# Encoder trunk on one core: next head's queries and the first attention projection moved ahead of the recurrences

## The chip, the cores and the metric

One core of one Trainium2 chip runs the whole kernel. The metric is the device time in microseconds (us) of one execution; three timed runs stand for the kernel before, and one further execution was profiled. TensorE is PE, its weight load PEld, VectorE DVE, ScalarE ACT, GpSimd POOL, SyncE SP.

## What is computed

Two layers, 1024 positions of width 1024, fp32. The reference, cut:

```python
def hybrid_layer(x, ...):
    proj = rms_norm(x, norm1_g) @ w_in
    mq, mk, mv, mo, mi, mf, aq, ak, av = split(proj)
    mq, mk = silu(centred_depthwise_conv([mq, mk], conv_w))       # width 5
    # mLSTM, 4 heads x 128: one chunkwise scan forward, one backward, summed
    hm = mlstm_chunkwise(q, k, v, gi[0], log_sigmoid(gf[0])) + flip(mlstm_chunkwise(flip(...)))
    y_m = head_rms_norm(hm) * head_norm_g * sigmoid(mo)
    # attention, 8 heads x 64: rotary q and k, windows (128,1) (512,4) (2048,16), merged
    y_a = dilated_attention(rope(aq), rope(ak), av)
    x = x + [y_m, y_a] @ w_out
    u = relu(rms_norm(x, norm2_g) @ w_up)
    return x + (u * u) @ w_down
```

## The kernel before, in words

**Matmuls.** Everything is kept transposed: 128 features on the partitions, 1024 positions along the free dimension, in two halves of 512. Each fp32 product is three matmuls of split operands, a high part and a residue (`mm3`, L85 to L92): `wh` with `hh`, `wh` with `hl`, `wl` with `hh`. Weights come by DMA in tiles `wr` of four 128x128 blocks; `wsplit` (L76) has ScalarE cast the high part `wh` (L80) and GpSimd subtract it, which leaves the residue `wl` (L82). There are three buffers each of `wr`, `wh` and `wl`. One projection to 128 features (`proj`, L184) needs two such tiles and is 48 matmuls of 128x512, in two PSUM banks (`pj`, at times `pm`).

**mLSTM** (L291 to L442, called from `layer`, L692). For each of the four heads: `m_proj` projects q and k and lets each go through a width-5 convolution (ScalarE's first product, L317; four VectorE passes over 128x1024, L319) and SiLU (L335, L337), transposes v, and projects the output gate `so` (L339 its sigmoid). `m_values` projects the v of the next head; head 0's was made with the gates. `m_head` fetches two broadcasts per direction by DMA (L351 to L358), makes the decay matrix E from them (L353, L355), transposes k (L369, copied to `kn`, L371), makes the scores (L376) and multiplies them into E (L378, VectorE); then it runs the recurrence over 8 chunks in both directions (L392, L394, L403; VectorE updates the state C, L406 and L408). `m_tail` normalises the head before, transposes it (L438) and multiplies it into `y`. The transposes, the scores and the recurrence's updates share two PSUM banks, tag `s`.

**Attention** (from L452). After the four heads `a_kq` projects k and then q of the first pair of heads, with the rotation on VectorE and GpSimd (`rope`, L462 to L469); it is a generator, and each step is three matmuls. v follows. Then there is `a_pair` for each of four pairs: 8 turns T of scores, softmax, transposes (L639) and products; between them `fill(n)` draws n steps of the next pair's projections, so that TensorE has work while VectorE and ScalarE make the softmax.

**Output projection and feed-forward** use seven products of block sums (Strassen's scheme), with `products` (L831): four weight tiles `w`, each 12 matmuls over four k-tiles whose operands are in `parts`: `parts[0]` holds k-tiles 0 and 1, `parts[1]` 2 and 3. The operands of the output projection's first product are casts `b<-y` (L792) of the results `y`.

**Order of the work.** A scheduler places the instructions on each engine's queue; its priority is the program's order, raised by 400 for weight splits and PSUM evacuations, and `issue_after` ties an instruction behind another one. In `a_pair` PE keeps the written order (`in_order`). Each engine then runs its queue in order, and waits for the others by semaphores.

Of the kernel before, what the change touches and what calls it, by code (L numbers as in the profile page):

```python
# [19 lines left out]
P = 128  # L20
# [23 lines left out]
class Trunk:  # L44
# [152 lines left out]
    def gates(self, L, hs, acc, pl, order):  # L197
# [3 lines left out]
        ws = self.ws0 or [self.wload(self.a["w_in"][L, 0, :, 4 * i:4 * i + 4]) for i in range(2)]  # L201
        yield
# [3 lines left out]
        self.ws0 = None  # L206
# [84 lines left out]
    def m_values(self, L, h, hs, r, mp):  # L291
# [8 lines left out]
        return zv, v1  # L300

    def m_proj(self, L, h, hs, r, mp, gates, values):

        nc = self.nc
        base = 1 + 4 * h
        zv, v1 = values
        qk = []
        for i in range(2):
            ps = self.proj(L, base + 1 + i, hs)
            z = mp.tile([P, S + 4], F32, name="z", tag="z", bufs=3)  # L310
            nc.gpsimd.memset(z[:, 0:2], 0.0)
            nc.gpsimd.memset(z[:, S + 2:S + 4], 0.0)
            for t in range(2):
                self.evac_r(z[:, 2 + t * HALF:2 + (t + 1) * HALF], ps[t], r, t)
            c = mp.tile([P, S], F32, name="c", tag="qk", bufs=4)
            cw = self.cw[:, L, i * MH + h]
            nc.scalar.activation(c, z[:, 0:S], AF.Copy, scale=cw[:, 0:1])  # L317
            for j in range(1, 5):
                nc.vector.scalar_tensor_tensor(out=c, in0=z[:, j:j + S], scalar=cw[:, j:j + 1], in1=c,  # L319
                                               op0=ALU.mult, op1=ALU.add)  # L320
            qk.append(c)
            if i == 1:
                next(gates, None)
            else:
                for g in range(2):
                    pt = self.mx.tile([P, 4, P], F32, name="pt", tag="s", bufs=2)
                    for c in range(4):
                        nc.tensor.transpose(pt[:, c], zv[:, (4 * g + c) * P:(4 * g + c + 1) * P], self.ident)
                    nc.scalar.copy(v1[:, 4 * g:4 * g + 4, 0:P], pt)
        so = mp.tile([P, S], F32, name="so", tag=f"so{h % 2}", bufs=1)  # L330
        ps = self.proj(L, base, hs)
# [3 lines left out]
        last = nc.scalar.activation(qk[1], qk[1], AF.Silu)  # L335
        with self.tc.issue_after(last.ins):
            last = nc.scalar.activation(qk[0], qk[0], AF.Silu)  # L337
# [253 lines left out]
    def a_pair(self, p, qkv, ops, ap, more, nxt=None):  # L591
# [58 lines left out]
        if p == 0:  # L650
            fill(8)
            v1, v23 = self.a_vt(qkv[2], ap, fill)
# [560 lines left out]
```

## Time and profile before

| | us |
|---|---|
| three runs, median (lowest to highest) | 2574.28 (2572.6 to 2579.54) |
| profiled execution, whole time | 2581.37 |
| its span in the trace | 2579.6 |
| busy in it: PE, PEld | 2451.5, 1954.0 |
| busy in it: DVE, ACT, POOL | 1897.8, 1241.0, 1342.9 |

The span holds what the trace shows of the execution; the rest of the whole time lies around it. Layer 0's mLSTM is at about 25 to 282 us, its attention to 582, the output projection from there; in layer 1 the mLSTM lies at 1275 to 1553, the attention from 1594, the output projection from 1858. A row of the timeline gives the start, the duration, and in brackets the time for which the engine was idle before it, with what ended that wait. The granted clock is a share of full speed, 2.4 GHz.

### The profile page before, as it was taken

To read this page: it belongs to the slowest core of one execution; us is meant where nothing else is said; L and a number is where in the kernel's file an instruction comes from. 1 tells how busy PE (TensorE), PEld (TensorE's weight loads), DVE (VectorE), ACT (ScalarE), POOL (GpSimd) and SP (SyncE) were. 2 spreads that over 40 slices of the span, in tenths; PEclk is the share of its full clock that TensorE was granted. 3 is DMA by queue.
4 is the path that set the end of the run, shared out by engine and by line. 5 is a ranking of instruction groups with operands and counts; after the bars stand their busy time and mean duration, and the time that the engine had idled before them with its cause. 6 is when DMAs were issued, how large, how long until landed. Compare 5 with 4: busy or idle time off the path is not lost. (4 is left out here: it accounts for less than half of the span.)

```text
span 2579.6 us, 35988 instructions
## 1 busy us (share of the span) xinstructions
PE 2451.5 (95%) x13470; PEld 1954.0 (76%) x13470; DVE 1897.8 (74%) x2388; ACT 1241.0 (48%) x2068; POOL 1342.9 (52%) x1111
## 2 busy tenths in 40 slices
PE   8999989998999999999998999999999999999997
PEld 6788766666788788787787887666677787887876
DVE  6576766778886766968766666667787968778687
ACT  5444444455544545454543443445466455454554
POOL 4232323336676667767642324223366767667765
PEclk9999999999999999999999999999999999999998
DMA  4432100154565555655333221003454555545553
GB/s 146 120 88 85 39 22 26 46 144 109 104 108 113 107 106 103 111 107 122 90 107 102 86 82 36 21 25 95 107 119 95 110 107 112 115 101 106 111 102 82
DMA packets 136288, 239.65 MB, mean 93 GB/s; under 512 B 15009, under 2 KB 34481, under 8 KB 136113
## 3 DMA queue, kind: packets, MB, share of 16 engines
q0 software_dynamic: 49216, 101.45, 23.5%
q1 hardware_dynamic: 86896, 135.89, 17.1%
q8 instruction: 107, 1.75, 0.3%
q14 instruction: 69, 0.56, 0.1%
HBM read 228.50 MB, written 8.65 MB: 92 GB/s over the span
## 5 line engine op out<-in xcount | busy, mean ns | idle before, releaser
L82 POOL TENSOR_TENSOR wl<-w,wh 128x512 fp32r<-128x512 f32 x484 | 774.0, 1619 | 287.7 <-ACT wh L80 286.7
L846 PE MATMUL ph<-b,wh 128*128 128x512 f32 x2240 | 692.8, 391 | 2.0 <-ACT wh L80 2.0
L80 ACT CAST wh<-w 128x512 fp32r<-128x512 f32 x484 | 297.9, 618 | 401.7 <-POOL wl L82 121.7
L846 PEld LDWEIGHTS ph<-b,wh 128*128 128x128 f32 x2240 | 421.6, 188 | 90.9 <-ACT wh L80 3.9
L846 PE MATMUL ph<-b,wl 128*128 128x512 f32 x1120 | 440.9, 394 | 14.9 <-POOL wl L82 14.5
L82 POOL TENSOR_TENSOR wl<-wr,wh 128x512 fp32r<-128x512 f32 x132 | 197.3, 1496 | 395.0 <-ACT wh L80 365.4
L846 PE MATMUL pj<-b,wh 128*128 128x512 f32 x1224 | 381.2, 393 | 9.3 <-ACT wh L80 4.7
L793 DVE TENSOR_TENSOR b<-T,b 128x1024 fp32r<-128x1024 f32 x144 | 248.4, 1729 | 122.6 <-ACT b L792 119.0
L90 PE MATMUL pj<-hh,wh 128*128 128x512 f32 x768 | 312.9, 407 | 0.6 <-ACT wh L80 0.6
L92 PE MATMUL pj<-hh,wl 128*128 128x512 f32 x768 | 301.7, 393 | 0.2 <-POOL wl L82 0.2
L91 PE MATMUL pj<-hl,wh 128*128 128x512 f32 x768 | 301.5, 393 | 0.0
L846 PEld LDWEIGHTS pj<-b,wh 128*128 128x128 f32 x1224 | 231.6, 190 | 60.5 <-ACT wh L80 5.6
L846 PEld LDWEIGHTS ph<-b,wl 128*128 128x128 f32 x1120 | 210.9, 188 | 71.1 <-POOL wl L82 28.2
L846 PE MATMUL pj<-b,wl 128*128 128x512 f32 x612 | 241.1, 394 | 11.1 <-POOL wl L82 11.1
L90 PEld LDWEIGHTS pj<-hh,wh 128*128 128x128 f32 x768 | 145.2, 189 | 44.3 <-issue 16.8
L792 ACT CAST b<-T 128x1024 fp32r<-128x1024 f32 x144 | 151.4, 1051 | 50.5 <-DVE T L808 17.1
L92 PEld LDWEIGHTS pj<-hh,wl 128*128 128x128 f32 x768 | 145.0, 189 | 32.2 <-POOL wl L82 1.3
L91 PEld LDWEIGHTS pj<-hl,wh 128*128 128x128 f32 x768 | 145.1, 189 | 27.1 <-issue 0.5
L820 POOL DMA_DIRECT2D w<-w_down x128 | 117.0, 946 | 73.4 <-DMA w<-w_down 27.2
L626 ACT ACTIVATE sm<-sm,nm 128x512 f32<-128x512 f32 x128 | 91.6, 717 | 127.9 <-DVE nm L624 127.9
L846 PEld LDWEIGHTS pj<-b,wl 128*128 128x128 f32 x612 | 116.0, 190 | 39.1 <-POOL wl L82 15.1
L820 POOL DMA_DIRECT2D w<-w_up x128 | 113.5, 908 | 61.6 <-POOL wl L82 22.9
(264 smaller groups left out, 4383.1 us busy)
## 6 DMA issues: line engine op xcount, KB each, us to landing
w<-w_up SPq DMA_DIRECT2D x128, 256.0 KB, 2.7
w<-w_up POOLq DMA_DIRECT2D x128, 256.0 KB, 4.1
w<-w_down SPq DMA_DIRECT2D x128, 256.0 KB, 2.7
w<-w_down POOLq DMA_DIRECT2D x128, 256.0 KB, 4.2
wr<-w_in SPq DMA_DIRECT2D x116, 256.0 KB, 2.7
E<-cm SPq DMA_DIRECT2D x16, 512.0 KB, 6.1
qi<-gd SPq DMA_DIRECT2D x16, 512.0 KB, 7.4
E<-gd POOLq DMA_DIRECT2D x16, 512.0 KB, 7.5
```

Of the source, the lines that this page charges most:

```text
L80: self.split = nc.scalar.copy(wh, raw).ins
L82: nc.gpsimd.tensor_tensor(out=wl, in0=raw, in1=wh.bitcast(F32), op=ALU.subtract)
L90: nc.tensor.matmul(ps, wh[:, j, :], xh[:, sl], start=start, stop=False)
L91: nc.tensor.matmul(ps, wh[:, j, :], xl[:, sl], start=False, stop=False)
L92: nc.tensor.matmul(ps, wl[:, j, :], xh[:, sl], start=False, stop=stop)
L626: nc.scalar.activation(sm, sm, AF.Exp, scale=-1.0, bias=nm, accum_out=l)
L792: nc.scalar.copy(hi, src)
L793: nc.vector.tensor_tensor(out=lo, in0=src, in1=hi.bitcast(F32), op=ALU.subtract)
L820: self.nc.gpsimd.dma_start(w, src, accum_op=ALU.add)
L846: nc.tensor.matmul(out, a[:, k, :], b, start=new and k + i == 0, stop=k + i == 5, skip_group_check=not new)
```

## The change

It has five parts. (1) `m_first` takes the place of `m_values`: beside the next head's v it projects the next head's q, with q's convolution and the transposes of v, and it is called before `m_head`; `m_proj` keeps k and the gate. (2) For the last head the first 16 steps of `a_kq`, the k projection of the first pair, are drawn before `m_head`. (3) In the first pair, `fill(8)` ahead of the transposes of v becomes `fill(6)`, and turns 0 to 2 draw 5 steps where they drew 4. (4) The output projection's first products run over `parts[0]` for three weight tiles and then over `parts[1]` (`late`). (5) Layer 1's gate weights are loaded and split ahead of the norm in the program's order.

```diff
@@ -198,12 +198,10 @@
 
         nc = self.nc
         ps = [self.mx.tile([P, HALF], F32, name="ps", tag="s", bufs=2) for _ in range(2)]
-        ws = self.ws0 or [self.wload(self.a["w_in"][L, 0, :, 4 * i:4 * i + 4]) for i in range(2)]
-        yield
+        ws = self.ws0
         for k in order:
             for t in range(2):
                 self.mm3(ps[t], ws[k // 4], k % 4, hs[k], t, k == order[0], k == order[-1])
-        self.ws0 = None
         ws = [self.wload(self.a["w_in"][L, 4, :, 4 * i:4 * i + 4]) for i in range(2)]
         self.ahead = self.pj2(True)
         for t in range(2):
@@ -288,7 +286,24 @@
         yield
 
 
-    def m_values(self, L, h, hs, r, mp):
+    def m_conv(self, L, h, i, hs, r, mp):
+
+        nc = self.nc
+        ps = self.proj(L, 2 + 4 * h + i, hs)
+        z = mp.tile([P, S + 4], F32, name="z", tag="z", bufs=3)
+        nc.gpsimd.memset(z[:, 0:2], 0.0)
+        nc.gpsimd.memset(z[:, S + 2:S + 4], 0.0)
+        for t in range(2):
+            self.evac_r(z[:, 2 + t * HALF:2 + (t + 1) * HALF], ps[t], r, t)
+        c = mp.tile([P, S], F32, name="c", tag="qk", bufs=4)
+        cw = self.cw[:, L, i * MH + h]
+        nc.scalar.activation(c, z[:, 0:S], AF.Copy, scale=cw[:, 0:1])
+        for j in range(1, 5):
+            nc.vector.scalar_tensor_tensor(out=c, in0=z[:, j:j + S], scalar=cw[:, j:j + 1], in1=c, op0=ALU.mult,
+                                           op1=ALU.add)
+        return c
+
+    def m_first(self, L, h, hs, r, mp):
 
         nc = self.nc
         ps, self.ahead = self.ahead or self.proj(L, 4 + 4 * h, hs), None
@@ -297,48 +312,32 @@
             self.evac_r(zv[:, t * HALF:(t + 1) * HALF], ps[t], r, t)
         v1 = mp.tile([P, NC, P + 1], F32, name="v1", tag=f"v1{h % 2}", bufs=1)
         nc.gpsimd.memset(v1[:, :, P:P + 1], 1.0)
-        return zv, v1
-
-    def m_proj(self, L, h, hs, r, mp, gates, values):
-
-        nc = self.nc
-        base = 1 + 4 * h
-        zv, v1 = values
-        qk = []
-        for i in range(2):
-            ps = self.proj(L, base + 1 + i, hs)
-            z = mp.tile([P, S + 4], F32, name="z", tag="z", bufs=3)
-            nc.gpsimd.memset(z[:, 0:2], 0.0)
-            nc.gpsimd.memset(z[:, S + 2:S + 4], 0.0)
-            for t in range(2):
-                self.evac_r(z[:, 2 + t * HALF:2 + (t + 1) * HALF], ps[t], r, t)
-            c = mp.tile([P, S], F32, name="c", tag="qk", bufs=4)
-            cw = self.cw[:, L, i * MH + h]
-            nc.scalar.activation(c, z[:, 0:S], AF.Copy, scale=cw[:, 0:1])
-            for j in range(1, 5):
-                nc.vector.scalar_tensor_tensor(out=c, in0=z[:, j:j + S], scalar=cw[:, j:j + 1], in1=c,
-                                               op0=ALU.mult, op1=ALU.add)
-            qk.append(c)
-            if i == 1:
-                next(gates, None)
-            else:
-                for g in range(2):
-                    pt = self.mx.tile([P, 4, P], F32, name="pt", tag="s", bufs=2)
-                    for c in range(4):
-                        nc.tensor.transpose(pt[:, c], zv[:, (4 * g + c) * P:(4 * g + c + 1) * P], self.ident)
-                    nc.scalar.copy(v1[:, 4 * g:4 * g + 4, 0:P], pt)
+        q = self.m_conv(L, h, 0, hs, r, mp)
+        for g in range(2):
+            pt = self.mx.tile([P, 4, P], F32, name="pt", tag="s", bufs=2)
+            for c in range(4):
+                nc.tensor.transpose(pt[:, c], zv[:, (4 * g + c) * P:(4 * g + c + 1) * P], self.ident)
+            nc.scalar.copy(v1[:, 4 * g:4 * g + 4, 0:P], pt)
+        return q, v1
+
+    def m_proj(self, L, h, hs, r, mp, gates, first):
+
+        nc = self.nc
+        q, v1 = first
+        k = self.m_conv(L, h, 1, hs, r, mp)
+        next(gates, None)
         so = mp.tile([P, S], F32, name="so", tag=f"so{h % 2}", bufs=1)
-        ps = self.proj(L, base, hs)
+        ps = self.proj(L, 1 + 4 * h, hs)
         for t in range(2):
             self.evac_r(so[:, t * HALF:(t + 1) * HALF], ps[t], r, t)
         next(gates, None)
-        last = nc.scalar.activation(qk[1], qk[1], AF.Silu)
+        last = nc.scalar.activation(k, k, AF.Silu)
         with self.tc.issue_after(last.ins):
-            last = nc.scalar.activation(qk[0], qk[0], AF.Silu)
+            last = nc.scalar.activation(q, q, AF.Silu)
         with self.tc.issue_after(last.ins):
             last = nc.scalar.activation(so, so, AF.Sigmoid)
         self.tables(last)
-        return qk[0], qk[1], so, v1
+        return q, k, so, v1
 
     def m_head(self, L, h, prj, nat, mp, pend):
         nc = self.nc
@@ -648,7 +647,7 @@
             return p1s
 
         if p == 0:
-            fill(8)
+            fill(6)
             v1, v23 = self.a_vt(qkv[2], ap, fill)
         sms = weights(0)
         if p > 0:
@@ -662,7 +661,7 @@
                 ahead = weights(T + 1)
             if late:
                 take1(*late)
-            fill((5 if p > 0 else 4) if not last else 3)
+            fill((5 if p > 0 or T < 3 else 4) if not last else 3)
             if T % 4 == 0:
                 o1 = self.mx.tile([P, 4, P], F32, name="o1", tag="o", bufs=1)
             late = T, o1, turn(T, sms)
@@ -693,6 +692,9 @@
         tc, nc, a = self.tc, self.nc, self.a
         self.L = L
         order = (0, 1, 2, 3, 4, 5, 6, 7) if L == 0 else (1, 3, 5, 7, 0, 2, 4, 6)
+        if L > 0:
+            with self.tc.issue_after(self.fetched.ins):
+                self.ws0 = [self.wload(a["w_in"][L, 0, :, 4 * i:4 * i + 4]) for i in range(2)]
         hs, acc = self.norm(xT, self.g1[:, L], order, L)
         if L > 0:
             for d in range(KD):
@@ -703,14 +705,12 @@
                 self.order(mp, (("z", S + 4, 3), ("so0", S, 1), ("v10", S + NC, 1), ("so1", S, 1),
                                 ("v11", S + NC, 1), ("qk", S, 4), ("G", S + 2 * NC, 7)))
                 gates = self.gates(L, hs, acc, mp, order)
-                with self.tc.issue_after(self.fetched.ins) if L > 0 else nullcontext():
-                    next(gates)
                 r, nat = next(gates)
-                pend, values = None, self.m_values(L, 0, hs, r, mp)
+                pend, first = None, self.m_first(L, 0, hs, r, mp)
                 for h in range(MH):
-                    prj = self.m_proj(L, h, hs, r, mp, gates, values)
+                    prj = self.m_proj(L, h, hs, r, mp, gates, first)
                     if h < MH - 1:
-                        values = self.m_values(L, h + 1, hs, r, mp)
+                        first = self.m_first(L, h + 1, hs, r, mp)
                     if h == MH - 1:
                         cos = self.nrm.tile([P, S], F32, name="cos", tag="r", bufs=2)
                         tabs = [[cos[:, t * HALF:(t + 1) * HALF] for t in range(2)],
@@ -720,10 +720,12 @@
                                 sl = slice(t * HALF, (t + 1) * HALF)
                                 nc.gpsimd.dma_start(tabs[i][t], a["rope"][:, i, sl])
                                 nc.gpsimd.tensor_tensor(out=tabs[i][t], in0=tabs[i][t], in1=r[:, sl], op=ALU.mult)
+                        qkv, ps, last = [self.ya(n) for n in ("qq", "kk")], [], []
+                        kq = self.a_kq(L, 0, hs, tabs, qkv[1], qkv[0], mp, "z", 3, last)
+                        for _ in range(16):
+                            next(kq)
                     pend = (L, h, prj, nat, self.m_head(L, h, prj, nat, mp, pend), mp)
-                qkv, ps = [self.ya(n) for n in ("qq", "kk")], []
-                last = []
-                for _ in self.a_kq(L, 0, hs, tabs, qkv[1], qkv[0], mp, "z", 3, last):
+                for _ in kq:
                     pass
                 last[0]()
                 more = self.a_proj(L, 3 + 4 * MH, hs, ps)
@@ -828,11 +830,12 @@
             return self.pj.tile([P, HALF], F32, name="pj", tag="pj", bufs=3)
         return self.dn.tile([P, HALF], F32, name="pi", tag="pi", bufs=1)
 
-    def products(self, ws, parts, chain=False, ps=None, then=None):
+    def products(self, ws, parts, chain=False, ps=None, then=None, late=False):
+
 
         nc = self.nc
         new = ps is None
-        res = []
+        res, rest = [], []
         for q, w in enumerate(ws):
             out = self.bank(chain) if new else ps[q]
             wh, wl = self.wsplit(w)
@@ -840,11 +843,21 @@
                 self.third = self.split
             if then:
                 then(q)
-            for k in range(4):
-                hi, lo = [x[:, k % 2] for x in parts[k // 2]]
-                for i, (a, b) in enumerate(((wh, hi), (wh, lo), (wl, hi))):
-                    nc.tensor.matmul(out, a[:, k, :], b, start=new and k + i == 0, stop=k + i == 5,
-                                     skip_group_check=not new)
+            def half(j, wh=wh, wl=wl, out=out):
+                hi, lo = parts[j]
+                for k in range(2):
+                    for i, (a, b) in enumerate(((wh, hi), (wh, lo), (wl, hi))):
+                        nc.tensor.matmul(out, a[:, 2 * j + k, :], b[:, k], start=new and j + k + i == 0,
+                                         stop=j + k + i == 4, skip_group_check=not new)
+
+            half(0)
+            if late and q < 3:
+                rest.append(half)
+            else:
+                half(1)
+            if q == 2:
+                for x in rest:
+                    x(1)
             res.append(out)
         return res
 
@@ -879,7 +892,7 @@
             for q in range(4):
                 addto(w2, 1, 1)(q)
             take(1, chain)
-        ps = self.products(w1, op)
+        ps = self.products(w1, op, late=early)
         w1 = self.fetch("w1", src, 1, 1)
         for j in range(2):
             self.nc.vector.tensor_tensor(out=T[j], in0=B11[j], in1=B12[j], op=ALU.subtract)
```

What becomes of it on the engines' queues, at the three places of which the prediction speaks. The changed program's line numbers are lower by 1 to 17 up to L692 and higher after that.

PE, layer 0, head 0, from the last projection ahead of the recurrence to the recurrence's first matmuls. Before (L369 transposes of k, L376 scores, L392 and L403 recurrence):

```order
L92 MATMUL pj<-hh,wl 128x512
L369 MATMUL pt<-ident,c 128x128 x8
L90 MATMUL pm<-hh,wh 128x512
L376 MATMUL pt<-c 128x128 x8
L392 MATMUL pn<-v_381,E 128x129 x2
L91 MATMUL pm<-hl,wh 128x512
L403 MATMUL pk<-wv,kn 128x129
```

After (L319 transposes of the next head's v, L368 of k, L375 scores, L391 and L402 recurrence; L90 to L92 are k of the next head):

```order
L319 MATMUL pt<-ident,zv 128x128 x8
L90 MATMUL pj<-hh,wh 128x512
L368 MATMUL pt<-ident,c 128x128 x4
L91 MATMUL pj<-hl,wh 128x512
...
L368 MATMUL pt<-ident,c 128x128 x4
L375 MATMUL pt<-c 128x128 x8
L90 MATMUL pj<-hh,wh 128x512
L91 MATMUL pj<-hl,wh 128x512
L391 MATMUL pn<-v_381,E 128x129 x2
```

Ahead of these rows the queue held 48 matmuls of v in the old order and holds 96 of v and q now. Behind the rows, 16 matmuls of k and one L402 stand ahead of the other direction's first L391.

DVE, the same head, from the evacuation of v to the recurrence's state updates. Before (L378 the E multiplies, L440 the tail's product, L406 and L408 the state):

```order
L182 TENSOR_TENSOR zv<-pj,r 128x512 x2
L378 SCALAR_TENSOR_TENSOR E<-pt,E 128x512 x4
L440 SCALAR_TENSOR_TENSOR y<-pt,hg,so 128x512 x2
L406 COPY C<-pk 128x129 x2
L408 SCALAR_TENSOR_TENSOR C<-C,dec,pk 128x129 x12
```

After (L302 the convolution passes of the next head's q, L377 the E multiplies):

```order
L182 TENSOR_TENSOR zv<-pj,r 128x512 x2
L182 TENSOR_TENSOR z<-pm,r 128x512
L182 TENSOR_TENSOR z<-pj,r 128x512
L302 SCALAR_TENSOR_TENSOR c<-z,cw,c 128x1024 x2
L377 SCALAR_TENSOR_TENSOR E<-pt,E 128x512
L302 SCALAR_TENSOR_TENSOR c<-z,cw,c 128x1024
L377 SCALAR_TENSOR_TENSOR E<-pt,E 128x512
L302 SCALAR_TENSOR_TENSOR c<-z,cw,c 128x1024
L377 SCALAR_TENSOR_TENSOR E<-pt,E 128x512 x2
```

The four passes over q stand between the multiplies. At head 3 there is no next q; there the six rotation instructions of the attention's k (two each of L461, L462 and L468) stand ahead of the four multiplies.

ACT, at the end of layer 0's attention (`w` are weights of the output projection, `b` operands of its products, `B` and `acc` the next norm). Before:

```order
L792 CAST b<-y 128x1024
L80 CAST wh<-w_5587 128x512
L80 CAST wh<-w_5588 128x512
L80 CAST wh<-w_5589 128x512
L792 CAST b<-T 128x1024 x2
L80 CAST wh<-w_5590 128x512
L945 ACTIVATE B<-x_4828,g_116 128x512
L111 ACTIVATE acc<-x_4828 128x512
L80 CAST wh<-w_5571 128x512
```

After:

```order
L794 CAST b<-y 128x1024
L80 CAST wh<-w_5587 128x512
L80 CAST wh<-w_5588 128x512
L80 CAST wh<-w_5589 128x512
L794 CAST b<-T 128x1024 x2
L80 CAST wh<-w_5590 128x512
L958 ACTIVATE B<-x_4828,g_116 128x512
L80 CAST wh<-w_5571 128x512
L111 ACTIVATE acc<-x_4828 128x512
```

The first casts keep their order; of the next quarter's casts each stands one place earlier. At the start of layer 1 the rows of ACT, POOL and SP up to the gates' projections are the same in both programs.

## Rows read from the trace of the kernel before

**Rows 1.** The page: busy us, share of the span and instructions of each engine.
```profile
PE 2451.5 (95%) x13470; PEld 1954.0 (76%) x13470; DVE 1897.8 (74%) x2388; ACT 1241.0 (48%) x2068; POOL 1342.9 (52%) x1111
```
**Rows 2.** Chain of waits: a dense stretch of matmuls (start us, us, what).
```profile
1965.66 32.64 PE ph L846 x144
```
**Rows 3.** Timeline of PE, mLSTM of both layers (start us, us, what).
```profile
94.93 3.78 PE L376 MATMUL pt<-c 128*128 128x128 f32 x16 [4.10 <-ACT kn L371]
...
263.41 1.38 PE L369 MATMUL pt<-ident,c 128*128 128x128 f32 x8 [4.00 <-ACT c L335]
...
1367.10 3.42 PE L376 MATMUL pt<-c 128*128 128x128 f32 x16 [10.12 <-ACT kn L371]
...
1534.54 1.97 PE L369 MATMUL pt<-ident,c 128*128 128x128 f32 x8 [4.04 <-ACT c L335]
```
**Rows 4.** Timeline of ACT ahead of three of these waits.
```profile
262.30 1.06 ACT L335 ACTIVATE c<-c 128x1024 f32<-128x1024 f32 x1 [4.41 <-DVE c L319]
...
1360.97 1.06 ACT L355 ACTIVATE E<-E 128x1024 f32<-128x1024 f32 x1 [8.50 <-DVE E L353]
1361.93 0.60 ACT L80 CAST wh<-wr 128x512 fp32r<-128x512 f32 x1
...
1365.00 1.06 ACT L355 ACTIVATE E<-E 128x1024 f32<-128x1024 f32 x1 [1.86 <-DVE E L353]
...
1366.47 1.06 ACT L371 COPY kn<-pt 128x512 f32<-128x512 f32 x2
```
**Rows 5.** Windows (columns in the first line).
```profile
core 0: us, PE busy (x) PEld busy (x) DVE busy (x) ACT busy (x) POOL busy (x), PEclk, DMA share, GB/s
...
95.00:100.00 5.00, 5.00 (x22) 4.90 (x23) 2.54 (x4) 0.37 (x1) 0.74 (x1) 0.50 0.16 52
...
264.00:267.60 3.60, 3.47 (x17) 2.96 (x16) 3.27 (x3) 3.57 (x6) 1.81 (x1) 0.53 0.02 5
...
1367.00:1370.00 3.00, 2.90 (x13) 2.90 (x14) 0.72 (x2) 0.53 (x2) 0.90 (x1) 0.50 0.27 86
1534.50:1540.50 6.00, 5.96 (x26) 5.89 (x27) 4.75 (x6) 5.83 (x7) 1.80 (x1) 0.50 0.15 46
320.00:325.00 5.00, 3.22 (x22) 2.67 (x20) 2.95 (x4) 2.83 (x5) 4.81 (x3) 1.00 0.17 52
```
**Rows 6.** Line L317, ScalarE's first product (duration ns min/median/max).
```profile
L317 ACT ACTIVATE c<-z,cw x16: 1136/1152/1154, 56.5 to 1526.1; 128x1024 f32<-128x1024 f32 x16
```
**Rows 7.** Lines L319 and L378, groups of instructions (busy us, mean ns), timeline of DVE.
```profile
L319 DVE SCALAR_TENSOR_TENSOR c<-z,cw,c x64: 1271/1285/2404, 57.7 to 1532.1; 128x1024 f32<-128x1024 f32 x64
...
L378 DVE SCALAR_TENSOR_TENSOR E<-pt,E x32: 673/680/693, 97.1 to 1541.0; 128x512 f32<-128x512 f32 x32
...
L319 DVE SCALAR_TENSOR_TENSOR c<-z,cw,c 128x1024 f32<-128x1024 f32 x64 | 97.9, 1529 | 9.6 <-ACT c L317 8.3
...
130.33 7.06 DVE L319 SCALAR_TENSOR_TENSOR c<-z,cw,c 128x1024 f32<-128x1024 f32 x4
...
256.10 6.16 DVE L319 SCALAR_TENSOR_TENSOR c<-z,cw,c 128x1024 f32<-128x1024 f32 x4 [1.22 <-ACT c L317]
```
**Rows 8.** Timeline of PE, layer 0, head 1.
```profile
153.41 1.03 PE L369 MATMUL pt<-ident,c 128*128 128x128 f32 x8
...
154.68 2.05 PE L376 MATMUL pt<-c 128*128 128x128 f32 x16
```
**Rows 9.** Timeline of POOL.
```profile
131.82 4.49 POOL L82 TENSOR_TENSOR wl<-wr,wh 128x512 fp32r<-128x512 f32 x2 [4.74 <-PE pj L92]
...
1362.62 1.25 POOL L82 TENSOR_TENSOR wl<-wr,wh 128x512 fp32r<-128x512 f32 x1 [5.83 <-ACT wh L80]
```
**Rows 10.** Timelines of DVE and POOL: rotation of the attention's k, layer 0.
```profile
290.07 0.68 DVE L462 TENSOR_TENSOR kk<-pj,cos 128x512 f32<-128x512 f32 x1
...
290.67 0.73 DVE L463 STREAM_SHUFFLE rs<-pj 128x512 f32<-128x512 f32 x1
...
291.48 1.30 POOL L464 TENSOR_TENSOR rs<-rs,sin 128x512 f32<-128x512 f32 x1 [4.76 <-DVE v L431]
...
292.81 1.76 DVE L469 TENSOR_TENSOR kk<-kk,rs 128x512 f32<-128x512 f32 x1
...
330.75 0.68 DVE L469 TENSOR_TENSOR kk<-kk,rs 128x512 f32<-128x512 f32 x1
```
**Rows 11.** Timeline of PE, first pair of layer 0's attention.
```profile
322.13 0.97 PE L585 MATMUL pt<-ident,vt 128*128 128x128 f32 x5 [1.78 <-DVE v L587]
...
330.57 1.06 PE L639 MATMUL pt<-ident,sm 128*128 128x128 f32 x8 [1.42 <-DVE sm L628]
...
337.75 0.63 PE L639 MATMUL pt<-ident,sm 128*128 128x128 f32 x4 [0.64 <-DVE sm L628]
```
**Rows 12.** Timelines of ACT and PE, start of layer 0's output projection.
```profile
583.56 1.05 ACT L792 CAST b<-y 128x1024 fp32r<-128x1024 f32 x1 [7.85 <-DVE y L688]
...
585.18 1.22 PE L846 MATMUL pj<-b,wh 128*128 128x512 f32 x2 [2.33 <-ACT wh L80]
587.48 0.80 PE L846 MATMUL pj<-b,wl 128*128 128x512 f32 x1 [1.08 <-POOL wl L82]
```
**Rows 13.** Timeline of PE, layer 1's gates.
```profile
1282.19 0.50 PE L92 MATMUL ps<-hh,wl 128*128 128x512 f32 x1 [2.51 <-POOL wl L82]
...
1287.72 0.51 PE L92 MATMUL ps<-hh,wl 128*128 128x512 f32 x1 [1.87 <-POOL wl L82]
```

## The prediction

> **What bounds the kernel now.** I read the page's busy shares first. TensorE (PE) is busy 95% of the span [rows 1], and no other engine reaches 75%, so only PE's idle time and its time at half clock can be won. A dense 128x512 matmul takes 32.64/144 = 0.227 us [rows 2]; one projection is 48 of them, 10.9 us. Then I asked PE's timeline for idle time in the stages that the change touches. Four waits stand out, all in the mLSTM [rows 3]: 4.10 and 10.12 us ahead of head 0's scores (L376, layers 0 and 1), 4.04 and 4.00 us ahead of head 3's transposes of k (L369). Heads 1 and 2 have none. Together 22.26 us. ScalarE shows what ended them [rows 4]: at head 0 the copies kn (L371) stand behind the exponential E (L355), which waits for VectorE's E and so for E's DMAs; at head 3 the SiLU (L335) waits for the last convolution pass (L319).
>
> The windows behind these waits show a second loss [rows 5]: the granted clock is 0.50, which is 1.2 of 2.4 GHz, for 5.00 us of work in layer 0's head 0, 2.90 us in layer 1's, and 5.96 us at layer 1's head 3; 3.47 us at 0.53 at layer 0's. Half of that is lost: 2.5 + 1.45 + 3.0 + 1.7 = 8.65 us. So the four places cost 30.9 us.
>
> **The change part by part.** Every engine runs the same instructions as before; only their order moves. The sum is therefore waits removed against waits made.
>
> *q of the next head ahead of the recurrence.* Between output gate and recurrence PE had 48 matmuls of v; now it has 96. Layer 0's head 0: 10.9 us of work stand where the wait was 4.10 us, so it goes, with 2.5 us of half clock. Layer 1's head 0: v ends about 1355.6 (the wait begins at 1367.10 - 10.12 = 1356.98, behind 1.03 us of transposes and a matmul). The first half of q's weights is cast ahead, 5.4 us of work, to 1361.1. The second half's cast stands in ScalarE's order still behind the first E, at 1361.93, and ends 1362.53 [rows 4]; its residue is made by POOL some 1.3 us later [rows 9], and the third matmul wants it. PE waits 1.4 + 0.9 = 2.3 us. I count 7.8 us won and no clock back there (bounds 0 and 1.45).
>
> *What q's convolution delays.* Let T be the end of q's projection. VectorE must now do q's four convolution passes between the E multiplies, where four multiplies stood alone. ScalarE's first product takes 1.15 us [rows 6] and ends about T+2.4 (z is evacuated at T+1.0, and a copy of v stands ahead). Four passes at the mean of 1.53 us [rows 7] are 6.1, four multiplies at 0.68 are 2.7 [rows 7]: the last E is there at T+11.2. PE wants it for the recurrence's other direction behind 8 transposes of v (1.03), 8 of k (1.03) and scores (2.05) [rows 8], 24 matmuls of k as filler (5.4) and three or four small matmuls (0.7): T+10.2. A wait of 1.0 us for each of heads 0 to 2, 6.0 us in all. With all passes at the median 1.285 it is 0; with all at 2.40, the slowest [rows 7], 4.5 us.
>
> *The attention's k projection ahead of head 3's recurrence.* The same 10.9 us cover 4.00 and 4.04 us, since the SiLU comes no later than now; with them go 1.7 + 3.0 us of half clock. In exchange k's rotation stands ahead of head 3's multiplies on VectorE: for each half 0.68 + 0.73 us, 1.30 us on POOL, and an addition of 0.7 to 1.76 us [rows 10]. The second half begins when the first addition ends, about 1.0 us behind the projection's end; 0.68 + 0.73 + 1.30 + 0.68 and a first multiply of 0.68 bring the first E 5.2 us behind it, and PE wants it at 1.03 + 0.23 + 2.05 + 0.45 = 3.8. That is 1.4, with the handing over 1.7 us per layer (2.8 if an addition takes 1.76): 3.4 us lost. Behind the recurrence 48 matmuls less cover the tail's chain and the rotations; this wait is not in the trace. I take 0.5 us per layer; it can't exceed the 10.9 us that left.
>
> *Fills.* The first pair's turns T=0 and T=1 wait 1.42 and 0.64 us for VectorE [rows 11]. One more step is 3 x 0.227 = 0.68 us, so 0.68 + 0.64 = 1.3 us per layer go, 2.6 in all. The two steps fewer ahead of the transposes of v could lengthen the 1.78 us wait there [rows 11] by up to 1.36; I count none, because that wait is for a PSUM copy late in the group.
>
> *Halves in the output projection.* The first cast of three weights still stands behind `b<-y`, which waits for the last pair's y [rows 12], in the old order and the new. So the 2.33 us wait stays. Products by halves ask for the second and third residue 6 matmuls sooner each than now, while POOL makes them no sooner; behind them the casts of the next quarter move one place only. Bounds per layer: 1.08 us won (the second wait) and 2 lost. I take 1 us lost, 2 in all.
>
> *Gate weights of layer 1.* The waits of 2.51 and 1.87 us [rows 13] would be its gain, but no row of ScalarE, POOL or SP moves there: nothing.
>
> **Sum.** Won: 4.10 + 7.8 + 4.00 + 4.04 = 19.9, clock 2.5 + 1.7 + 3.0 = 7.2, fills 2.6: 29.7. Lost: 6.0 + 3.4 + 1.0 + 2.0 = 12.4. Net 17.3 us. The profiled execution took 2581.4 us, so its like would take 2564; it lies 7.1 us above the median of 2574.3. The median goes to **2557 us**, 0.7% less.
>
> **Rule against row.** Four convolution passes took 1.54 us each at 256.10 and 1.77 us each at 130.33, and there POOL's subtractions run at the same time, from 131.82 on [rows 7, 9], while E's multiplies stay between 673 and 693 ns throughout [rows 7]. The Trainium skill, "SBUF — State Buffer", section "Who interferes with whom", says that a VectorE instruction with two SBUF inputs contends with a GpSimd instruction that reads SBUF; a pass reads z and c there, a multiply only E, with its scores from PSUM. The rows agree. By that rule alone the change would put passes on the path of the recurrence while POOL still prepares weights for it, which is the third rival.
>
> **Rivals.**
> 1. *Nothing new waits.* The splits of the next weights lie ready when q ends, POOL is quiet then, each pass takes 1.285 us, rotation fits. The price of 12.4 falls to about 3, and layer 1's head 0 gets its clock back: -28, **2546 us**. For it: the passes' median. Against it: a mean of 1.53, and the rotation's chain crosses two engines twice. Chance 0.22.
> 2. *The two score banks in PSUM take over.* Transposes of v, of k and the scores now pass in turn through two banks, and each waits for a ScalarE copy; q's first product of 1.15 us stands among these copies, which PE's order doesn't know. Two turns of 0.8 us more at six heads cost 10 us: net -7, **2567 us**. For it: kn already ended the waits at head 0. Against it: filler matmuls stand between them. Chance 0.17.
> 3. *Slower: VectorE starves the recurrence.* Place: the multiplies of heads 0 to 2, both layers. A wait of w us there costs w, and, if the clock halves behind it as it did behind the four waits, some 1.7 us more. Without that term the change nets 23.3 us, so it turns at w = 23.3/6 - 1.7 = 2.2 us, a pass of about 1.85 us. At the slowest pass of 2.40, w is 4.5: 6 x 6.2 = 37, net +14, **2588 us**. For it: passes up to 2.40 exist. Against it: most of POOL's subtractions for the next weights are ordered before T, and a wait of 1.78 us left the clock at 1.00 [rows 5, 11]. Chance 0.08.
> 4. *It doesn't do what it says.* That holds for the gate weights and for the cast in the output projection, as counted. For q and k the order shows the move, so this is no case of its own.
>
> My own case, 2550 to 2564 us, has 0.53.
>
> **How the numbers follow.** A measurement of this kernel can tell about 0.3%, 7.7 us, from no change: faster is below 2566.6, slower above 2582.0. Faster: the forecast (0.53), the first rival (0.22) and a little of the second. Same: the rest of the second and the milder half of the third. Faster 0.77, same 0.17, slower 0.06. The range leaves out the third rival and the outermost of the others: 2540 to 2574.
>
> **What would show it.** Right: no wait over 1 us ahead of L375 in layer 0's head 0 nor ahead of L368 at head 3, granted clock 1.00 there (lines of the changed kernel); a wait near 2.3 us inside q's projection in layer 1's head 0, ended by the cast of wh; small waits ended by VectorE's E ahead of L391 at heads 0 to 2 (about 1 us) and 3 (1.7); the 2.33 us at the output projection and 2.51 us at layer 1's gates unchanged. Wrong: waits over 2 us at L391 with half clock behind them (third rival); waits ended by copies of kn or v ahead of L368 or L375 (second); or idle time near 4 us at the attention's start, where the 48 matmuls were taken from.

## The result and the profile after

The changed kernel takes **2561.62 us** (2559.29 to 2565.47, four runs) where the kernel before takes 2576.53 on the same chip: ratio 0.9944, interval 0.9923 to 0.9966, some 14 us less. 2557 was forecast, in a range of 2540 to 2574, and the sign and the size came true. The terms behind the sum did not, as the trace and the runs below show. The profiled execution's span is 2558.2 us (2579.6 before).

PE's timeline, same views as [rows 3, 11, 12, 13]; in brackets the wait and what ended it:

```profile
269.77 1.23 PE L391 MATMUL pn<-v,E 128*128 128x129 f32 x4 [4.76 <-DVE E L377]
...
303.21 1.97 PE L437 MATMUL pt<-ident,H 128*128 128x128 f32 x8 [4.09 <-DVE H L432]
...
332.41 0.63 PE L638 MATMUL pt<-ident,sm 128*128 128x128 f32 x4 [0.52 <-DVE sm L627]
...
370.10 1.06 PE L638 MATMUL pt<-ident,sm 128*128 128x128 f32 x8 [1.34 <-DVE sm L627]
...
576.03 0.73 PE L850 MATMUL pj<-b,wh 128*128 128x512 f32 x2 [2.33 <-ACT wh L80]
...
594.72 0.73 PE L850 MATMUL ph<-b,wh 128*128 128x512 f32 x2 [2.66 <-ACT wh L80]
...
1273.41 0.50 PE L92 MATMUL ps<-hh,wl 128*128 128x512 f32 x1 [2.51 <-POOL wl L82]
...
1353.44 0.50 PE L92 MATMUL pm<-hh,wl 128*128 128x512 f32 x1 [0.62 <-POOL z L295]
...
1531.25 1.11 PE L391 MATMUL pn<-v,E 128*128 128x129 f32 x4 [4.74 <-DVE E L377]
...
1563.67 1.54 PE L437 MATMUL pt<-ident,H 128*128 128x128 f32 x6 [4.06 <-DVE H L432]
```

All four waits of [rows 3] are gone; in layer 1's head 0 only 0.62 us of the 10.12 is left. No wait stands at L391 at heads 0 to 2. In their place are two new ones per layer, both at head 3: 4.76 and 4.74 us for VectorE's E ahead of the recurrence, 4.09 and 4.06 us for VectorE's H, the head's result, ahead of the tail's transposes. Layer 1's head 3 has a small third one, 1.17 us for ScalarE's copies kn ahead of the scores (L375). The first pair's waits (those of [rows 11], three more of 0.73, 1.24 and 2.58 us in later turns, and small ones) have shrunk from 9.1 to 2.6 us per layer, far more than by one step's 0.68 us in two turns. Two of those in later turns, in the kernel before:

```profile
363.81 0.63 PE L639 MATMUL pt<-ident,sm 128*128 128x128 f32 x4 [1.24 <-DVE sm L628]
...
378.36 1.22 PE L639 MATMUL pt<-ident,sm 128*128 128x128 f32 x8 [2.58 <-DVE l L627]
```

The output projection's first wait is the old 2.33 us, but its next quarter's waits 2.66 us. Layer 1's gates are as before.

The granted clock, columns as in [rows 5]:

```profile
269.80:276.00 6.20, 6.20 (x25) 5.48 (x26) 3.49 (x6) 0.39 (x1) 0.00 (x0) 0.56 0.00 0
276.00:284.80 8.80, 8.80 (x80) 8.75 (x79) 4.50 (x13) 5.55 (x16) 0.00 (x0) 1.00 0.01 2
...
303.00:312.00 9.00, 8.79 (x37) 7.59 (x38) 5.82 (x7) 5.49 (x10) 2.75 (x5) 0.83 0.23 73
```

Behind the new waits the mean clock of these stretches is 0.56 and 0.83: part of each runs at 1.2 GHz, the rest at 2.4 GHz. So each wait costs 1.5 to 2.7 us more than its row says (6.20 us x 0.44, 9.00 us x 0.17): 4.76 + 2.7 + 4.09 + 1.5 = 13 us in layer 0's head 3, where the wait of 4.00 us and its 1.7 of half clock were taken away.

**Why head 3 waits.** VectorE and POOL between k's rotation and the E multiplies, layer 0:

```profile
257.21 2.85 DVE L363 SCALAR_TENSOR_TENSOR qi<-c,qi 128x1024 f32<-128x1024 f32 x2
259.99 0.68 DVE L461 TENSOR_TENSOR kk<-pj,cos 128x512 f32<-128x512 f32 x1
...
264.05 1.75 DVE L468 TENSOR_TENSOR kk<-kk,rs 128x512 f32<-128x512 f32 x1 [2.72 <-POOL rs L463]
265.72 0.68 DVE L461 TENSOR_TENSOR kk<-pj,cos 128x512 f32<-128x512 f32 x1
...
268.42 0.69 DVE L468 TENSOR_TENSOR kk<-kk,rs 128x512 f32<-128x512 f32 x1 [1.37 <-POOL rs L463]
269.03 2.48 DVE L377 SCALAR_TENSOR_TENSOR E<-pt,E 128x512 f32<-128x512 f32 x4
```
```profile
261.51 1.28 POOL L82 TENSOR_TENSOR wl<-wr,wh 128x512 fp32r<-128x512 f32 x1 [3.66 <-ACT wh L80]
262.75 1.27 POOL L463 TENSOR_TENSOR rs<-rs,sin 128x512 f32<-128x512 f32 x1
263.97 1.29 POOL L82 TENSOR_TENSOR wl<-wr,wh 128x512 fp32r<-128x512 f32 x1
```

The rotation begins late, behind the two products `qi` (q times its decay); then VectorE idles 2.72 us for POOL, which makes a weight residue first, and 1.37 us for the second half. The first addition takes 1.75 us beside POOL's next residue, the second 0.69 beside none. The Trainium skill, "SBUF — State Buffer", section "Who interferes with whom", has a VectorE instruction with two SBUF inputs contend with a GpSimd instruction that reads SBUF; the addition has two, and these rows agree.

The second wait comes from the same queue. VectorE ahead of the tail's transposes (L432 makes the H for which PE waits until 303.21; L461 and L468 rotate the attention's q):

```profile
293.86 1.10 DVE L461 TENSOR_TENSOR qq<-pj,cos 128x512 f32<-128x512 f32 x1
...
297.00 2.16 DVE L468 TENSOR_TENSOR qq<-qq,rs 128x512 f32<-128x512 f32 x1
299.01 1.04 DVE L461 TENSOR_TENSOR qq<-pj,cos 128x512 f32<-128x512 f32 x1
...
300.96 2.20 DVE L432 TENSOR_TENSOR H<-H,v 128x1024 f32<-128x1024 f32 x1
```

With k's 48 matmuls gone from behind the recurrence, q's projection ends sooner, and most of q's rotation stands ahead of H. In k_0_steps (below) it stands behind (L432 at 291.78 us, L461 at 292.92), and PE has no wait there.

At heads 0 to 2, where the passes over the next head's q stand among the E multiplies, no wait comes up. Head 1 of layer 0:

```profile
157.82 2.60 DVE L302 SCALAR_TENSOR_TENSOR c<-z,cw,c 128x1024 f32<-128x1024 f32 x2 [1.42 <-ACT c L300]
160.34 0.68 DVE L377 SCALAR_TENSOR_TENSOR E<-pt,E 128x512 f32<-128x512 f32 x1
160.94 1.28 DVE L302 SCALAR_TENSOR_TENSOR c<-z,cw,c 128x1024 f32<-128x1024 f32 x1
```

These passes take 1.28 to 1.30 us, not the mean of 1.53: between 157.5 and 164 us POOL, with the next weights already split, runs nothing, and the multiplies come in time.

### The profile page after: what moved, and what is told of

Same layout as the page of the kernel before. It is cut to its first block, busy times and chain, and to the rows that moved or that the text cites. A ratio compares the mean times of both kernels' runs of the same rounds, so it can differ in the third digit from the quotient of the medians.

```text
span 2558.2 us, 36007 instructions
## 1 busy us (share of the span) xinstructions
PE 2444.3 (96%) x13470; PEld 1949.3 (76%) x13470; DVE 1872.0 (73%) x2388; ACT 1245.8 (49%) x2068; POOL 1324.4 (52%) x1111
## 5 line engine op out<-in xcount | busy, mean ns | idle before, releaser
L82 POOL TENSOR_TENSOR wl<-wr,wh 128x512 fp32r<-128x512 f32 x132 | 185.6, 1407 | 436.1 <-ACT wh L80 371.8
L90 PE MATMUL pj<-hh,wh 128*128 128x512 f32 x768 | 313.8, 409 | 0.6 <-ACT wh L80 0.6
L92 PE MATMUL pj<-hh,wl 128*128 128x512 f32 x768 | 302.9, 394 | 0.7 <-POOL wl L82 0.7
L90 PEld LDWEIGHTS pj<-hh,wh 128*128 128x128 f32 x768 | 145.8, 190 | 42.6 <-issue 15.8
L92 PEld LDWEIGHTS pj<-hh,wl 128*128 128x128 f32 x768 | 145.1, 189 | 31.4 <-POOL wl L82 1.6
L80 ACT CAST wh<-wr 128x512 fp32r<-128x512 f32 x132 | 80.2, 613 | 144.8 <-PE pj L91 102.0
```

What stands on the lines that cost most here:

```text
L80: self.split = nc.scalar.copy(wh, raw).ins
L82: nc.gpsimd.tensor_tensor(out=wl, in0=raw, in1=wh.bitcast(F32), op=ALU.subtract)
L90: nc.tensor.matmul(ps, wh[:, j, :], xh[:, sl], start=start, stop=False)
L92: nc.tensor.matmul(ps, wl[:, j, :], xh[:, sl], start=False, stop=stop)
```

## The experiments

All ratios are to the kernel before on the same chip, with 95% intervals. The runs lie on three chips: the first four rows on one; k_8_kn_first, q_only, fills_old and halves_off on another; the rest on a third. Runs of different chips are compared by their ratios.

| run | median us | ratio | interval |
|---|---|---|---|
| changed_again | 2558.96 | 0.9947 | 0.9934 to 0.9959 |
| k_0_steps | 2551.16 | 0.9917 | 0.9904 to 0.9930 |
| k_8_steps | 2563.93 | 0.9965 | 0.9954 to 0.9977 |
| k_15_steps | 2553.30 | 0.9922 | 0.9909 to 0.9934 |
| k_8_kn_first | 2551.08 | 0.9900 | 0.9887 to 0.9914 |
| q_only | 2557.16 | 0.9924 | 0.9911 to 0.9936 |
| fills_old | 2576.06 | 0.9998 | 0.9987 to 1.0009 |
| fills_only | 2567.05 | 0.9970 | 0.9959 to 0.9981 |
| halves_off | 2554.44 | 0.9913 | 0.9899 to 0.9927 |
| halves_only | 2583.85 | 1.0027 | 1.0015 to 1.0039 |
| best | 2543.39 | 0.9873 | 0.9860 to 0.9886 |
| best_8_ahead | 2550.20 | 0.9899 | 0.9886 to 0.9912 |

**How much of k goes ahead of head 3.** Four runs on one chip: the changed kernel, and

```diff
-                        for _ in range(16):
+                        for _ in range(0):    # k_0_steps; 8 in k_8_steps, 15 in k_15_steps
```

> The changed kernel once more, on the same chip as the three variants. Expected as measured: 2561.6 us, 0.9944 of the kernel before. In the profile the two new waits at head 3 (4.76 and 4.74 us at L391 for VectorE's E) and at its tail (4.09 and 4.06 us at L437 for VectorE's H).

> No step of the attention's k projection ahead of head 3 (this part of the change undone, the rest kept). Theory 1: the waits at L391 and at the tail's L437 vanish, the old wait of 4.0 us with its half clock (1.7 and 3.0 us) comes back at L368: against the changed kernel about -26 + 13 = -13 us, 2549 us; that is, this part of the change as it stands costs time. Theory 2: the backlog takes the gain back: about 2562 us, no difference.

> Only 8 of the 16 steps of the attention's k projection are drawn ahead of head 3's recurrence (24 matmuls, 5.4 us, still more than the wait of 4.0 us that they cover); the other 24 and k's rotation stay behind it. Theory 1 (both new waits come from this one part: the rotation stands ahead of the E multiplies, and the tail lost 48 matmuls of cover): both waits vanish in both layers, 9.5 + 8.2 us, with up to 8 us of half clock behind them; the wait of 4.0 us at L368 does not come back. Against the changed kernel -18 to -26 us, about 2536 to 2544 us. Theory 2 (the waits only give VectorE time to work off its backlog, so that the attention's first turns lose again what is won here): the first pair's waits grow from 2.6 to about 9 us per layer as before, and the gain against the changed kernel is 5 to 13 us, 2549 to 2557 us.

> 15 of 16 steps drawn: the same cover ahead of head 3, but the last three matmuls and k's rotation come behind the E multiplies. Theory 1: the wait at L391 (4.76 and 4.74 us) with its half clock (2.7 and 1.7 us) vanishes, the wait at the tail's L437 stays near 4 us: -12 to -14 us against the changed kernel, about 2549 us. If the wait at L391 came from the scores or kn instead of the rotation, it would stay and the time would be 2561 us.

Without the part the kernel is 7.8 us faster than with it (2551.16 against 2558.96; the intervals don't meet): as it stands this part costs time. Its waits on PE are then these, and none at L391 or L437:

```profile
257.34 1.09 PE L368 MATMUL pt<-ident,c 128*128 128x128 f32 x8 [3.31 <-ACT c L334]
...
315.07 0.79 PE L584 MATMUL pt<-ident,vt 128*128 128x128 f32 x5 [3.17 <-DVE v L586]
...
1515.56 1.97 PE L368 MATMUL pt<-ident,c 128*128 128x128 f32 x8 [4.68 <-ACT c L334]
```

The old waits are back, and the attention's first waits didn't grow beyond the 3.17 us: theory 1, less a part that the transposes of v take. With 15 steps the wait at L391 is gone, so the rotation made it, not the scores or kn. The gain of 5.7 us is half of what was expected: PE comes to the tail sooner, so the wait there grew to 5.70 and 5.67 us, and a wait of 0.87 us per layer for the state C came up. With 8 steps both theories missed: 2563.93 us, slower than 0, 15 and 16 steps. Both waits are gone there, but a third has come:

```profile
266.60 3.57 PE L375 MATMUL pt<-c 128*128 128x128 f32 x16 [4.46 <-ACT kn L370]
```
```profile
261.78 1.28 ACT L338 ACT_TABLE_LOAD   x1
263.08 1.06 ACT L338 ACTIVATE so<-so 128x1024 f32<-128x1024 f32 x1
264.15 1.28 ACT L58 ACT_TABLE_LOAD   x1
265.44 0.62 ACT L80 CAST wh<-wr 128x512 fp32r<-128x512 f32 x1
265.97 1.07 ACT L370 COPY kn<-pt 128x512 f32<-128x512 f32 x2
```

ScalarE's order now has the copies kn behind the sigmoid and its two table loads; PE, there sooner than the order had reckoned with, waits 4.46 us, and behind the recurrence another 2.37 us for VectorE's shuffle `rs` (4.47 and 2.38 us in layer 1). With 0 steps the copies stand ahead of sigmoid and table loads. With 16 they stand behind them too, but PE comes later and waits only in layer 1, 1.17 us.

**That order mended.** Head 3's sigmoid is tied behind the copies:

```diff
+        if h == MH - 1:
+            with self.tc.issue_after(last.ins):      # last: the second copy kn
+                last = nc.scalar.activation(so, so, AF.Sigmoid)
+            self.tables(last)
```

> 8 steps drawn ahead of head 3, and head 3's sigmoid with its two table loads tied behind the copies kn on ScalarE. In the run with 8 steps the copies stood behind sigmoid and table loads (1.28 + 1.06 + 1.28 us) and PE waited 4.46 and 4.47 us for them ahead of the scores. Theory 1 (that order on ScalarE alone made 8 steps slower than 0): the wait ahead of the scores falls under 1 us, and the time is that of 8 steps less 9 us and 3 to 4 us of half clock, about 2551 us, or a little below 0 steps (2551.2), since the waits of 3.3 and 4.7 us at k's transposes are covered here. Theory 2 (PE reaches the scores too early, and another wait, for E or for C, takes its place): no faster than 2558 us.

2551.08 us, 0.9900: theory 1. The wait ahead of the scores is 1.02 us in layer 0 and under 0.5 in layer 1, that for E 1.57 us in each, and the one for `rs` is gone. So 8 steps in this order beat 16 in the old one (16 steps with the sigmoid tied were not run), and are no worse than none: the intervals of 0.9900 and 0.9917 overlap.

**Each part by itself.**

```diff
 q_only: range(0), fill(8), turns of 4 steps, no late=early
 fills_old: the changed kernel with
-            fill(6)   ...   fill((5 if p > 0 or T < 3 else 4) if not last else 3)
+            fill(8)   ...   fill((5 if p > 0 else 4) if not last else 3)
 halves_off: the changed kernel with
-        ps = self.products(w1, op, late=early)
+        ps = self.products(w1, op)
 fills_only, halves_only: the kernel before with the new lines of these two
```

> Only the first part of the change (and the gate weights, whose order did not move): q of the next head ahead of the recurrence, no steps of the attention's k, old fills, no halves. Theory: the waits of 4.10 and 10.12 us at head 0 vanish with 2.5 and 1.45 us of half clock, no wait at L391 takes their place: -17 to -18 us against the kernel before, 2555 us; the waits at k's transposes of head 3 (4.00, 4.04) and the first pair's (9.1 per layer) stay. Rival (a part only works together with the others: VectorE's late work goes into the attention): -8 us or less, 2565 us.

> The changed kernel with the old fills (8 steps ahead of the transposes of v, 4 in each turn). The prediction's term: 1.3 us per layer, so +2.6 us, 2561.6 us. Theory 1 from the trace of the changed kernel, whose waits in the first pair fell from 9.1 to 2.6 us per layer: the redealt fills move also where the next pair's rotations fall on VectorE, so the waits of 0.73, 1.24 and 2.58 us come back too: +8 to +13 us, 2567 to 2572 us. Theory 2 (these waits fell because PE's new wait at head 3's tail gave VectorE time): no difference beyond the prediction's 2.6 us.

> The kernel before with the redealt fills alone. Prediction's term: -2.6 us, 0.999. By the pair of the changed kernel with new and old fills: -10 to -13 us, about 0.9955; the waits of 0.73, 1.24 and 2.58 us in the first pair vanish, the 1.78 us at the transposes of v grows to about 3.1.

> The changed kernel without the halves: the output projection's first products in the old order. The prediction's term: 1 us per layer lost by the halves, so -2 us here, 2557 us; the stage's idle time, 13.7 and 13.3 us in the changed kernel against 11.8 and 12.2 before, goes back. If the longer wait of 2.64 us at the next quarter's cast (1.16 and 0.89 before) comes from elsewhere (the residues or VectorE), nothing changes: 2559 us.

> The kernel before with the halves alone. Prediction's term: 1 us per layer lost, +2 us, no measurable difference. By the pair of the changed kernel with and without halves: +8 us, 1.003.

q alone gives 0.76%, 19.6 us, all that its theory asked for and 2 us more; 1.5 of the 2 us are shorter waits at head 3's transposes of k, 3.20 and 3.37 us where 4.00 and 4.04 were. The fills give 0.30% alone, 7.7 us, less than the 10 us expected; taken out of the changed kernel they cost 0.51% by the two ratios (0.9998 against 0.9947), 13 us. That they are worth several times the forecast 2.6 us is clear, the exact figure is not. The halves cost 0.27% alone and 0.34% in the changed kernel. The three parts multiply to 0.9924 x 0.9970 x 1.0027 = 0.9921, and k_0_steps, which is just these three, measures 0.9917: they add up.

*Why the fills are worth more.* VectorE in one turn of the first pair, old fills (fills_old) and then new (changed_again); L627 scales the softmax of the two heads, L461 and L462 rotate the next pair's q:

```profile
351.26 0.49 DVE L627 TENSOR_SCALAR sm<-sm,l 128x512 f32<-128x512 f32 x1
351.67 1.12 DVE L461 TENSOR_TENSOR qq<-pj,cos 128x512 f32<-128x512 f32 x1
...
353.50 0.49 DVE L627 TENSOR_SCALAR sm<-sm,l 128x512 f32<-128x512 f32 x1
```
```profile
351.53 0.49 DVE L627 TENSOR_SCALAR sm<-sm,l 128x512 f32<-128x512 f32 x1
...
352.13 0.49 DVE L627 TENSOR_SCALAR sm<-sm,l 128x512 f32<-128x512 f32 x1
352.61 1.12 DVE L461 TENSOR_TENSOR qq<-pj,cos 128x512 f32<-128x512 f32 x1
```

The order of VectorE's queue hangs on when a projection's steps end. With the old fills the rotation stands between the two heads' softmax, and PE waits 0.73 us for the second; with the new ones it stands behind both. In the same way the next turn's wait of 1.23 us goes. The last turn's wait only shrinks, from 2.59 to the 1.34 us above, and for another reason: ahead of its softmax stands an addition for the next pair's keys (L549), which takes 3.86 us with the old fills, where POOL starts a weight residue beside it, and 2.62 with the new:

```profile
371.30 3.86 DVE L549 TENSOR_TENSOR ks<-kk,ks 64x1024 fp32r<-64x1024 f32 x1
...
376.02 1.22 PE L638 MATMUL pt<-ident,sm 128*128 128x128 f32 x8 [2.59 <-DVE l L626]
```
```profile
368.56 2.62 DVE L549 TENSOR_TENSOR ks<-kk,ks 64x1024 fp32r<-64x1024 f32 x1
```

In return the transposes of v wait 3.15 us in fills_only where they waited 1.78 and 1.85 before: 1.37 and 1.30 us more, for two missing steps of 1.36 us. In the changed kernel they wait for nothing with either fills, as in k_15_steps: all of these have the wait for H ahead of them, and k_0_steps, which lacks it, has 3.17 us there. So the fills cost nothing at this place in the changed kernel, which is part of why they are worth more in it.

*Why the halves cost more.* The output projection of layer 0 from its first matmul to a later one that has the same number of matmuls ahead of it in either order (218 in the trace), with halves (changed_again) and without (halves_off):

```profile
579.12:641.83 62.71, 55.26 (x218) 43.24 (x219) 50.62 (x43) 34.46 (x53) 39.48 (x33) 0.92 0.50 111
```
```profile
580.12:639.33 59.21, 53.45 (x218) 42.27 (x218) 48.87 (x45) 35.16 (x55) 39.61 (x33) 0.94 0.52 117
```

The same work takes 3.50 us longer; in layer 1 it is 62.80 against 59.28 us, 3.52. Together that is 7.0 us, all that the halves cost alone. About half is waiting (7.45 against 5.76 us of PE idle), the rest the same matmuls at a lower clock (0.92 against 0.94). The largest wait is for the next quarter's cast, 2.64 us against 1.04. It leads to VectorE, with halves and then without (L865 adds the first product to x; L958 is ScalarE's next use of x, behind which the cast stands):

```profile
593.41 2.35 DVE L810 SCALAR_TENSOR_TENSOR T<-y,T 128x1024 f32<-128x1024 f32 x2
595.68 1.27 DVE L865 TENSOR_TENSOR x<-x,pj 128x512 f32<-128x512 f32 x2
596.39 0.72 ACT L958 ACTIVATE B<-x,g 128x512 f32<-128x512 f32 x1 [7.24 <-DVE x L865]
```
```profile
593.78 0.68 DVE L865 TENSOR_TENSOR x<-x,pj 128x512 f32<-128x512 f32 x1
594.37 2.35 DVE L810 SCALAR_TENSOR_TENSOR T<-y,T 128x1024 f32<-128x1024 f32 x2
594.49 0.72 ACT L958 ACTIVATE B<-x,g 128x512 f32<-128x512 f32 x1 [4.99 <-DVE x L865]
```

By halves the first product is complete later, so its addition to x falls behind the operands T, and ScalarE's cast comes 2.4 us later counted from the first matmul (597.02 and 595.64). The rows show this chain; no run moves that one addition by itself.

**A version that beats both.** 8 steps with kn ahead, new fills, no halves; and the same with 8 steps ahead of the transposes of v and 5 in turns 0 and 1 alone.

> 8 steps with the copies kn ahead of the sigmoid, and no halves in the output projection. If the two gains add (0.9900 of the kernel before, and 0.9913 against 0.9947 for the halves taken out): 0.987, about 2542 us. If the halves cost only the 1 to 2 us of idle time that the trace shows per layer: about 0.989, 2547 us.

> As the one before, with 8 steps ahead of the transposes of v again and 5 steps in turns 0 and 1 alone. If the wait of 3.15 us at the transposes of v is the old one of 1.78 us and the two missing steps (2 x 0.68 us): it falls to about 1.8 us, 2.7 us less over both layers, provided the later waits of the first pair (0.52, 1.34) stay; if it is the place of the next pair's rotations that counts, some of 0.73, 1.24 and 2.58 us come back and nothing is won or up to 5 us lost.

The first takes 2543.39 us, 0.9873: the two gains add, 19 us below the changed kernel by the ratios. The second is 0.26% slower, 6.8 us, a little more than the expected 5: its wait at the transposes of v fell only to 2.77 us, and waits of 0.76, 0.85, 0.75 and 1.07 us came up in and behind the turns. At the first two a rotation, here of the next pair's k, again stands ahead of the softmax on VectorE (L466 at 320.42 us, L632 at 321.84).

## Why the prediction was right, and where it was not

The total was right by luck: its errors cancelled. By parts, in us (forecast; measured by the ratio of the part's own run, and for k as the difference of changed_again and k_0_steps):

| part | forecast | measured |
|---|---|---|
| q ahead (heads 0, with the wait at heads 0 to 2) | -8.4 | -19.6 |
| k ahead of head 3 | -8.3 | +7.8 |
| fills | -2.6 | -7.7 |
| halves | +2.0 | +7.0 |
| gate weights | 0 | not run alone; its waits of 2.51 and 1.87 us are unchanged |

- *q ahead.* The mechanism held: 10.9 us of work closed 4.10 and nearly all of 10.12. Two terms were too dark. "A wait of 1.0 us for each of heads 0 to 2" was 0: the pass was priced at a mean that includes slow passes beside POOL's residues, and here POOL is idle. And the 2.3 us left in layer 1's head 0 were 0.62, ended on POOL and not by the cast, with no half clock there: the first E came 1.7 us sooner, counted from the gates' start (80.2 us against 81.9). Of this 0.9 us is VectorE's, whose four passes over head 0's q took 6.23 us where they had taken 7.14; the rest is open.
- *k ahead of head 3.* The step that failed is "that is 1.4, with the handing over 1.7 us per layer" (its terms add up to 5.1, not 5.2 us, which changes little). It measured 4.75. I let the rotation begin when its own projection was done and POOL be free; in the queues it stands behind the two `qi` products on VectorE and a residue on POOL, and its first addition ran contended. The other is "I take 0.5 us per layer" for the tail, which measured 4.1: the 48 matmuls that left had covered VectorE's chain up to H (division, norm), and now q's rotation stands in it. The prediction's last part named this place, with the right size, as a sign of being wrong, and the sum had it at 0.5. Half clock behind both (1.5 to 2.7 us each) was not priced at all.
- *Fills.* The term counted a step as 0.68 us of cover (work that fills a wait), and only the waits of turns 0 and 1; the 0.73, 1.24 and 2.58 us of later turns were left out, and it is these that the new place in VectorE's order removed or shortened. "I count none" for the transposes of v failed in fills_only, where the full 1.3 us came.
- *Halves.* The wait of 2.33 us stayed, as forecast; the loss of 1 us per layer was 3.5. The forecast looked at the residues and at ScalarE's order, and not at the addition to x on VectorE for which that order waits.
- *Rivals.* The third didn't come: the passes among the multiplies took 1.27 to 1.30 us (the slow ones, up to 2.33 us, lie elsewhere), and there was no wait at L391 at heads 0 to 2. Of the second the changed kernel has the 1.17 us for kn in layer 1; large waits for kn came in k_8_steps alone, where the copies stand behind a table load and not in a turn of the two banks. The fourth held for the gate weights.

## What to carry to other kernels

Price a moved step by the queue it lands in, on every engine that it crosses, and ask what was hidden by it where it stood: cover moved from one wait to another is not won twice, and here half as much of it, with one ScalarE order mended, gave more than all of it. A change of several parts with a small net deserves a run of each part: two of these lost time, and the ratios of the other two multiply to 0.9924 x 0.9970 = 0.9894, about twice the gain of the whole (these two together were not run). Where a scheduler decides the order, a count of matmuls can act through another engine's queue.

## What the runs showed of the hardware

- The clock's answer to a wait is not the same each time. In k_0_steps PE waits 3.17 us for the same copy in both layers' attention, in each after more than 11 us without a gap at a granted clock of 1.00. Behind the wait the mean granted clock is 0.75 in layer 0 (some of it at 1.2 GHz) and 1.00, all at 2.4 GHz, in layer 1:

```profile
315.10:322.00 6.90, 6.90 (x44) 5.48 (x45) 2.48 (x8) 1.82 (x5) 2.73 (x2) 0.75 0.14 42
...
1574.40:1581.00 6.60, 6.60 (x48) 5.07 (x49) 3.33 (x10) 2.27 (x6) 2.74 (x2) 1.00 0.16 50
```

So half clock behind a new wait of this kernel is priced with both ends, 0 and some 3 us (5.96 us at 0.50 in [rows 5]).
- An addition of two SBUF operands over 128x512 took 0.69 us alone and 1.75 us beside POOL's subtraction, 2.5 times as much.
